# Loading ScalarE's activation tables ahead, and queueing four SiLUs later, in a one-core decoder layer

## The chip, the cores and the metric

The kernel runs on one core of one Trainium2 chip. The metric is the device time of one execution in microseconds (us): a kernel's time is the median of several runs, and beside it there is one execution taken by the hardware profiler. The core's engines each have an instruction queue of their own that is worked off in order: TensorE (PE, matrix products), VectorE (DVE), ScalarE (ACT, activation functions and copies), GpSimd (POOL) and SyncE (SP, which here issues the DMA transfers). They meet only through semaphores.

## The reference, cut to what matters

One decoder layer over 1024 tokens of width 1024. One input projection gives all streams and a SiLU gate for each of three branches; the gated branches go through one output projection and a layer norm.

```python
z = x @ w_in[layer]
u_a, v_a, g_a, x_b, g_b, q_x, g_x = jnp.split(z, SPLITS, axis=-1)
y_a = spatial_gating(gelu(u_a), gelu(v_a), ...)
y_b = s5_branch(x_b, ...)                       # state-space layer; sin/cos tables, gelu, sigmoid
y_x = memory_cross_attention(q_x, mem, w_k, w_v)   # softmax over 256 memory tokens
y = concatenate([y_a * silu(g_a), y_b * silu(g_b), y_x * silu(g_x)])
x = layer_norm(DN_ALPHA * x + y @ w_out[layer], ln_g[layer], ln_b[layer])
```

Seven streams, then: sin, silu, exp, gelu and sigmoid are all computed on ScalarE, at different times.

## The kernel before

Every large product is done as three fp32r products: each operand is split into a high part, cast by ScalarE (`S.copy`, line 65), and a low part, the rest, subtracted by VectorE (line 62). `piece` loads 256 KB of a weight into a `raw` buffer (4 of them, `NRAW`) and splits it into a `hi` and a `lo` buffer (6 of each, `NPC`).

The order of the work is fixed in two ways. TensorE's order is always that of the program text. For VectorE, ScalarE and GpSimd there are two kinds of stretches, opened by `ordered`: in an "a" stretch these three also keep the order of the text among themselves; in a "p" stretch the tool that builds the program orders them from a simulated timeline, and what is written in a "p" stretch may also be queued ahead of instructions of the "a" stretch before it. SyncE's issues are always ordered by that tool. Small generators (`spawn`, `launch`, `tick`) interleave the side work in the text.

The stages that matter here, in order:

1. The gate of the attention branch (`gx`, four PSUM banks of pool `psu`) and the queries (`q`, four banks of pool `psz`) are computed together over eight k-steps (lines 526 to 546, an "a" stretch). Beside them `ssm_params` prepares the state-space parameters, with two Sin activations (lines 432, 433). In the last step `kv.fetch()` splits the first two pieces of the memory weights (`wk`, `wv` twice), and as soon as a gate is complete, SiLU moves it from PSUM into `yx` (line 544). Then `q_evac` moves the queries: ScalarE writes the upper copy, VectorE the rest (lines 247 and 250).
2. The memory keys and values (`KV.run`, lines 277 to 307) use the same four `psu` banks that SiLU has emptied. From here on it is a "p" stretch. There are four weight pieces of `wk` and `wv`; the third and fourth are split while the products run.
3. The products `xb` and `gb` run while 16 attention units (`s_unit`, lines 560 to 615) are interleaved with them: scores `s`, the negated row maximum `nm` (VectorE), Exp (ScalarE, line 576), the reciprocal `ri` and the scaling (VectorE, lines 580 and 582), transposes `pt` (TensorE, line 587), their split (ScalarE and VectorE), and for each pair of units the product `av`, whose half is copied to `ot` by ScalarE (line 611). `gb` is moved to `yb` as it is (line 222), and `gb_silu` (line 805) applies SiLU to it in place later in the text, after the attention's end.
4. The remaining products (`v`, `u`, `ga`), the state-space batches, the output projection and the layer norm follow.

ScalarE holds one set of function tables at a time. The program builder puts an ACT_TABLE_LOAD ahead of an activation whose function isn't in the set that is loaded; the trace shows these loads as instructions of ScalarE, with the line of the activation that they serve. Plain copies and casts run under any set.

Of the kernel before, what the change touches and what calls it, by code (L numbers as in the profile page):

```python
# [9 lines left out]
F32 = mybir.dt.float32  # L10
# [3 lines left out]
AF = mybir.ActivationFunctionType  # L14
# [4 lines left out]
P = 128  # L19
# [17 lines left out]
def trunk_kernel(ctx, tc, xT, x, w_gq, w_kv, memT, w_fm, w_v, w_o,  # L37
# [3 lines left out]
    V, S, G, T = nc.vector, nc.scalar, nc.gpsimd, nc.tensor  # L41
# [6 lines left out]
    def ordered(kind):  # L48
        order_st.close()
        if sets[kind]:  # L50
            order_st.enter_context(tc.manual_schedule(engines=set(sets[kind])))
# [3 lines left out]
    def mul(eng, o, a, b):  # L55
        eng.tensor_tensor(o, a, b, op=ALU.mult)
# [11 lines left out]
    def open_pool(name, bufs=1, side="left", space=None):  # L68
        st = ExitStack()
        kw = dict(name=name, bufs=bufs)  # L70
        if space is not None:
            kw["space"] = space
        else:
            kw["side"] = side
        return st, st.enter_context(tc.tile_pool(**kw))

    dram_st, dpool = open_pool("xd", space=bass.MemoryType.DRAM)
    const_st, const = open_pool("const")
# [29 lines left out]
    def advance():  # L108
        while pending and gate[0] <= now[0]:
            gen, spacing = pending.pop(0)  # L110
            gate[0] = max(gate[0], now[0] - 4.0) + spacing
            active.append([now[0], gen])
        for job in list(active):
            if job[0] <= now[0]:
                lag = next(job[1], None)
                if lag is None:
                    active.remove(job)
                else:
                    job[0] = now[0] + lag

    def tick(cost):
        now[0] += cost
        advance()
# [18 lines left out]
    def mm3(ps, sh, sl, mh, ml, start, stop, chk=False):  # L142
        kw = dict(skip_group_check=True) if chk else {}
        T.matmul(ps, lhsT=sh, rhs=mh, start=start, stop=False, **kw)  # L144
        T.matmul(ps, lhsT=sh, rhs=ml, start=False, stop=False, **kw)  # L145
        T.matmul(ps, lhsT=sl, rhs=mh, start=False, stop=stop, **kw)  # L146
# [13 lines left out]
    yb = base.tile([P, 2, SEQ], F32, tag="yb", name="yb")  # L160
    tok = [slice(t * P, t * P + P) for t in range(8)]
    half = [slice(0, 512), slice(512, 1024)]
# [59 lines left out]
        return lambda h, ps: S.copy(dst[:, f, half[h]], ps)  # L222


    warm = const.tile([P, P], BF16, name="warm")
    V.memset(warm, 0.0)
    wps = zbank("warm")
# [14 lines left out]
    def q_evac():  # L242
        for f in range(2):
            for h in range(2):
                for hh in range(2):
                    src = qps[f][h][hh * 64:hh * 64 + 64]
                    S.activation(qs[0:64, 2 * f + hh, half[h]], src, AF.Copy, scale=0.125)
                for hh in range(2):
                    src = qps[f][h][hh * 64:hh * 64 + 64]
                    V.scalar_tensor_tensor(qs[64:128, 2 * f + hh, half[h]], src, 0.125,  # L250
                                           qs[0:64, 2 * f + hh, half[h]].bitcast(F32),
                                           op0=ALU.mult, op1=ALU.subtract)
# [96 lines left out]
    def ssm_params():  # L349
# [81 lines left out]
        yield 3.0  # L431
        S.activation(sn, ang, AF.Sin, scale=TWO_PI)
        S.activation(an2, ang, AF.Sin, scale=PI_LO)
        mul(V, an2, an2, an2)
        V.tensor_scalar(cn, an2, -2.0, 1.0, op0=ALU.mult, op1=ALU.add)
        yield 3.0
# [35 lines left out]
    kv = KV()  # L472
# [42 lines left out]
    def first_half(wt):  # L515
        def mm(f, w, x, a, b, start=False):
            T.matmul(fps[f][0][:, a:b], lhsT=wt[f][w], rhs=(xh, xl)[x][:, 0, a:b], start=start,
                     stop=False, skip_group_check=True)

        for w, x in ((0, 0), (1, 0), (0, 1)):  # L520
            for m, (a, b) in enumerate(cuts):
                mm(0, w, x, a, b, w + x + m == 0)
        for w, x in ((0, 0), (0, 1), (1, 0)):
            mm(1, w, x, 0, 512, w + x == 0)

    wts = [stage(0)]
    for kt in range(KT):
        wt = wts[kt]
        if kt < KT - 1:
            wts.append(stage(kt + 1))  # L530
        if kt == KT - 1:
            kv.fetch()
        for f in range(4):
            wh, wl = wt[f]
            if kt == 0 and f < 2:
                if f == 0:
                    first_half(wt)
                mm3(fps[f][1], wh, wl, xh[:, 0, half[1]], xl[:, 0, half[1]], True, False)
            else:
                mm3x2(fps[f], wh, wl, kt, kt == 0, kt == KT - 1,  # L540
                      skip=(0,) if f < 2 else ())
            if kt == KT - 1 and f < 2:
                for h in range(2):
                    S.activation(yx[:, f, half[h]], fps[f][h], AF.Silu)
        if kt < KT - 1:
            tick(5.2)
    q_evac()
    ordered("p")
    tick(5.2)
    run_units([kv], xb[0])  # L550
# [5 lines left out]
    ordered("p")  # L556
    att_st, att = open_pool("att", side="right")
    pts = {}

    def s_unit(lt, hp):  # L560
        ps = ubank(f"s{lt}{hp}")
        for hh in range(2):
            qt = qs[:, 2 * hp + hh, tok[lt]]
            pv = ps[:, hh * 256:hh * 256 + 256]
            T.matmul(pv, lhsT=qt, rhs=kh[:, 2 * hp + hh], start=hh == 0, stop=False,
                     skip_group_check=True)
            T.matmul(pv, lhsT=qt, rhs=kl[:, 2 * hp + hh], start=False, stop=hh == 1,
                     skip_group_check=True)
        now[0] += 0.43
        ps3 = ps.rearrange("p (h m) -> p h m", h=2)  # L570
        nm = att.tile([P, 2], F32, tag="nm", bufs=3, name=f"nm{lt}{hp}")
        V.tensor_reduce(nm, ps3, axis=AX.X, op=ALU.max, negate=True)
        pr = att.tile([P, 2, 256], F32, tag="pr", bufs=3, name=f"pr{lt}{hp}")
        rs = att.tile([P, 2], F32, tag="rs", bufs=3, name=f"rs{lt}{hp}")
        for h in range(2):
            S.activation(pr[:, h], ps3[:, h], AF.Exp, bias=nm[:, h:h + 1], scale=1.0,
                         accum_out=rs[:, h:h + 1])
        yield 2.5
        ri = att.tile([P, 2], F32, tag="ri", bufs=3, name=f"ri{lt}{hp}")
        V.reciprocal(ri, rs)  # L580
        for h in range(2):
            V.tensor_scalar(pr[:, h], pr[:, h], ri[:, h:h + 1], None, op0=ALU.mult)
        yield 1.3
        tp = ubank(f"pt{lt}{hp}")
        for h in range(2):
            for m in range(2):
                T.transpose(tp[:, (h * 2 + m) * P:(h * 2 + m) * P + P],
                            pr[:, h, m * P:m * P + P], ident)
        now[0] += 0.43
        lq, lr = lt // 2, lt % 2  # L590
        if lr == 0:
            pts[(lq, hp)] = (att.tile([P, 4, 256], F32R, tag="pth", bufs=2, name=f"pth{lq}{hp}"),
                             att.tile([P, 4, 256], F32R, tag="ptl", bufs=2, name=f"ptl{lq}{hp}"))
        ph, pl = pts[(lq, hp)]
        tp3 = tp.rearrange("p (a l) -> p a l", a=4)
        S.copy(ph[:, :, tok[lr]], tp3)
        sub(V, pl[:, :, tok[lr]], tp3, ph[:, :, tok[lr]].bitcast(F32))
        if lr == 1:
            yield 3.8
            ps = ubank(f"av{lq}{hp}")  # L600
            for h in range(2):
                for m in range(2):
                    for n, pp in enumerate((ph, pl)):
                        T.matmul(ps[:, h * 256:h * 256 + 256], lhsT=vs[:, m, 2 * hp + h],  # L604
                                 rhs=pp[:, h * 2 + m], start=h + m + n == 0,
                                 stop=h + m + n == 3, skip_group_check=True)
            now[0] += 0.87
            cs = slice(lq * 256, lq * 256 + 256)
            ot = att.tile([P, 256], F32, tag="ot", bufs=2, name=f"ot{lq}{hp}")
            for h in range(2):  # L610
                S.copy(ot[h * 64:h * 64 + 64], ps[64:128, h * 256:h * 256 + 256])
            for h in range(2):
                add(V, ot[h * 64:h * 64 + 64], ps[0:64, h * 256:h * 256 + 256],
                    ot[h * 64:h * 64 + 64])
            mul(V, yx[:, hp, cs], yx[:, hp, cs], ot)
# [22 lines left out]
    for hp in range(2):  # L638
        for lt in range(8):
# [7 lines left out]
                  lambda tt, ps, vb=vb: v_evac(vb, tt, ps), lambda vb=vb: v_done(vb))  # L647
# [157 lines left out]
    def gb_silu():  # L805
        for f in range(2):
            for h in range(2):
                S.activation(yb[:, f, half[h]], yb[:, f, half[h]], AF.Silu)
                yield 2.0

    gate[0] = now[0]
# [22 lines left out]
    def v_done(vb):  # L834
        spawn(mix_all(vb))
# [158 lines left out]
    for t in range(7):  # L994
        ps = zbank(f"o1{t}")
# [6 lines left out]
    for c in range(2):  # L1002
        ps = zbank(f"o17{c}")
# [86 lines left out]
```

## Time and profile before

| what | value |
|---|---|
| median of the runs | 397.46 us (3 runs: 397.12 to 398.84) |
| profiled execution | 398.77 us |
| its span, first to last instruction | 397.1 us |
| busy: PE, DVE, ACT, POOL | 381.8, 267.6, 158.2, 101.2 us |
| mean granted TensorE clock | 0.994 of full speed |

The profiled execution's own time is 1.67 us longer than its span, and 1.31 us above the median of the runs. Busy times add up instructions of one engine; the engines overlap. In the rows below, the number in brackets is the idle time of the engine before the instruction, with what ended it.

### The profile page before, as it was taken

To read this page: it belongs to the slowest core of one execution; us is meant where nothing else is said; L and a number is where in the kernel's file an instruction comes from. 1 tells how busy PE (TensorE), PEld (TensorE's weight loads), DVE (VectorE), ACT (ScalarE), POOL (GpSimd) and SP (SyncE) were. 2 spreads that over 40 slices of the span, in tenths; PEclk is the share of its full clock that TensorE was granted. 3 is DMA by queue.
4 is the path that set the end of the run, shared out by engine and by line. 5 is a ranking of instruction groups with operands and counts; after the bars stand their busy time and mean duration, and the time that the engine had idled before them with its cause. 6 is when DMAs were issued, how large, how long until landed. Compare 5 with 4: busy or idle time off the path is not lost.

```text
span 397.1 us, 5806 instructions
## 1 busy us (share of the span) xinstructions
PE 381.8 (96%) x2129; PEld 330.2 (83%) x2129; DVE 267.6 (67%) x579; ACT 158.2 (40%) x301; POOL 101.2 (25%) x80
## 2 busy tenths in 40 slices
PE   8999989899998999999999999999999999999990
PEld 7887888688886999888888999888888888888890
DVE  4579877788885778799769349754447311874475
ACT  4572496576778432323153223134356310012210
POOL 1305000000000493830954600310000000026773
PEclk9999999999999999999999999999999999999997
DMA  7873525221850100302011002400138710002124
GB/s 230 286 242 117 164 80 185 82 79 28 152 62 26 54 4 14 107 24 71 28 42 56 26 17 82 132 0 2 53 104 295 290 55 0 0 2 88 70 107 159
DMA packets 22189, 35.89 MB, mean 90 GB/s; under 512 B 5376, under 2 KB 8848, under 8 KB 22032
## 3 DMA queue, kind: packets, MB, share of 16 engines
q1 hardware_dynamic: 22160, 35.51, 29.3%
q8 instruction: 17, 0.28, 0.3%
q14 instruction: 12, 0.10, 0.1%
HBM read 29.67 MB, written 5.24 MB: 88 GB/s over the span
## 4 chain that ended last, share of the span: by engine, by line
PE 77%; DVE 7%; DMA 7%; ACT 5%; issue 2%; POOL 2%; SPq 0%; POOLq 0%; DVEq 0%; ACTq 0%
PE o L146 7%; PE o L145 7%; PE o L144 7%; DMA r_x<-in_xT_dram 5%; PE zv L146 4%; PE zv L145 4%; PE zv L144 4%; PE zu L151 4%; PE zu L152 4%; PE zg L151 4%; PE zu L154 4%; PE zg L152 4%; PE zg L154 4%; PE mx L858 2%; PE av L604 2%
## 5 line engine op out<-in xcount | busy, mean ns | idle before, releaser
L928 POOL TENSOR_TENSOR stat<-stat,nhalf 128x1 f32<-128x1 f32 x8 | 11.9, 1490 | 105.6 <-DVE stat L927 105.6
L146 PE MATMUL o<-h_wo,yl 128*128 128x512 f32 (+1 forms) x100 | 38.4, 384 | 0.0
L145 PE MATMUL o<-l_wo,yh 128*128 128x512 f32 (+1 forms) x100 | 38.4, 384 | 0.0
L144 PE MATMUL o<-h_wo,yh 128*128 128x512 f32 (+1 forms) x100 | 38.3, 383 | 0.0
L144 PE MATMUL zv<-h_v,xh 128*128 128x256 f32 x128 | 36.6, 286 | 0.0
L146 PE MATMUL zv<-h_v,xl 128*128 128x256 f32 x128 | 36.2, 283 | 0.0
L145 PE MATMUL zv<-l_v,xh 128*128 128x256 f32 x128 | 36.2, 283 | 0.0
L151 PE MATMUL zu<-xh,h_u 128*128 128x512 f32 x64 | 25.8, 404 | 0.0
L151 PE MATMUL zg<-xh,h_g 128*128 128x512 f32 x64 | 25.5, 399 | 0.0
L152 PE MATMUL zu<-xl,h_u 128*128 128x512 f32 x64 | 25.0, 391 | 0.0
L152 PE MATMUL zg<-xl,h_g 128*128 128x512 f32 x64 | 25.0, 390 | 0.0
L144 PEld LDWEIGHTS zv<-h_v,xh 128*128 128x128 f32 x128 | 24.5, 192 | 0.1
L145 PEld LDWEIGHTS zv<-l_v,xh 128*128 128x128 f32 x128 | 24.5, 192 | 0.1
L146 PEld LDWEIGHTS zv<-h_v,xl 128*128 128x128 f32 x128 | 24.5, 192 | 0.0
L937 ACT ACTIVATE res<-res,stat 128x1024 f32<-128x1024 f32 x6 | 6.9, 1157 | 41.1 <-POOL stat L928 41.1
L956 DVE SCALAR_TENSOR_TENSOR res<-res,o 128x512 f32<-128x512 f32 (+1 forms) x16 | 10.3, 646 | 19.2 <-PE o L146 19.2
L145 PEld LDWEIGHTS o<-l_wo,yh 128*128 128x128 f32 x100 | 18.8, 188 | 4.0
L144 PEld LDWEIGHTS o<-h_wo,yh 128*128 128x128 f32 x100 | 18.8, 188 | 3.9
L146 PEld LDWEIGHTS o<-h_wo,yl 128*128 128x128 f32 x100 | 18.8, 188 | 3.9
L154 PE MATMUL zu<-xh,l_u 128*128 128x512 f32 x64 | 19.8, 390 | 0.0
L154 PE MATMUL zg<-xh,l_g 128*128 128x512 f32 x64 | 19.7, 389 | 0.0
L665 POOL MEMSET M<- 128x512 f32 x2 | 1.0, 526 | 70.1 <-PE zgb L152 70.1
(300 smaller groups left out, 1077.9 us busy)
## 6 DMA issues: line engine op xcount, KB each, us to landing
r_wo<-in_w_o_dram SPq DMA_DIRECT2D x16, 256.0 KB, 2.9
res<-in_x_dram SPq DMA_DIRECT2D x8, 512.0 KB, 7.5
r_x<-in_xT_dram SPq DMA_DIRECT2D x15, 256.0 KB, 5.1
out_dram<-res SPq DMA_DIRECT2D x6, 512.0 KB, 2.6
r_v<-in_w_v_dram SPq DMA_DIRECT2D x8, 256.0 KB, 3.0
r_u<-in_w_fm_dram SPq DMA_DIRECT2D x8, 256.0 KB, 2.7
r_g<-in_w_fm_dram SPq DMA_DIRECT2D x8, 256.0 KB, 2.7
r_wgq<-in_w_gq_dram SPq DMA_DIRECT2D x7, 256.0 KB, 4.5
```

The lines of the kernel that those rows point to most:

```text
L144: T.matmul(ps, lhsT=sh, rhs=mh, start=start, stop=False, **kw)
L145: T.matmul(ps, lhsT=sh, rhs=ml, start=False, stop=False, **kw)
L146: T.matmul(ps, lhsT=sl, rhs=mh, start=False, stop=stop, **kw)
L151: T.matmul(ps[h], lhsT=wh, rhs=xh[:, kt, half[h]], start=first, stop=False, **kw[h])
L152: T.matmul(ps[h], lhsT=wh, rhs=xl[:, kt, half[h]], start=False, stop=False, **kw[h])
L154: T.matmul(ps[h], lhsT=wl, rhs=xh[:, kt, half[h]], start=False, stop=last, **kw[h])
L604: T.matmul(ps[:, h * 256:h * 256 + 256], lhsT=vs[:, m, 2 * hp + h], rhs=pp[:, h * 2 + m], start=h + m + n == 0, stop=h + m + n == 3, skip_ ...
L665: G.memset(t, 0.0)
L858: T.matmul(ps[:, tok[c]], lhsT=t[:, cq * 4 + c, tok[h]], rhs=wT[:, hd], start=(c == 0), stop=(c == 3), skip_group_check=True)
L928: G.tensor_tensor(rs, rs, nhalf[:, 0:1], op=ALU.pow)
L937: S.activation(ot, ot, AF.Copy, scale=rs)
L956: V.scalar_tensor_tensor(res[:, t, c0:c0 + w], res[:, t, c0:c0 + w], ALPHA, ps[:, :w], op0=ALU.mult, op1=ALU.add)
```

## The change

A two-column constant tile `dummy` and a helper `table(func)` are added: `table` runs one activation from the first column into the second, one element on each partition. It is called twice: with Silu, right behind the two Sin activations of `ssm_params`, and with Exp, right behind `q_evac` and still in the "a" stretch. In the last k-step only the first piece of the memory weights is split; the second follows behind the four SiLUs, ahead of `q_evac`. The four SiLUs of `g_b` get an edge in ScalarE's queue behind the last copy to `ot` of the attention.

```diff
+    dummy = const.tile([P, 2], F32, name="dummy")
+    V.memset(dummy, 0.0)
+
+    def table(func):
+
+        S.activation(dummy[:, 1:2], dummy[:, 0:1], func)
...
         S.activation(an2, ang, AF.Sin, scale=PI_LO)
+        table(AF.Silu)
...
         if kt == KT - 1:
-            kv.fetch()
+            kv.fetch(1)
...
             tick(5.2)
+    kv.fetch(2)
     q_evac()
+    table(AF.Exp)
     ordered("p")
...
+    last_att = [None]
...
             for h in range(2):
-                S.copy(ot[h * 64:h * 64 + 64], ps[64:128, h * 256:h * 256 + 256])
+                last_att[0] = S.copy(ot[h * 64:h * 64 + 64], ps[64:128, h * 256:h * 256 + 256])
...
             for h in range(2):
-                S.activation(yb[:, f, half[h]], yb[:, f, half[h]], AF.Silu)
+                with tc.issue_after(last_att[0].ins):
+                    S.activation(yb[:, f, half[h]], yb[:, f, half[h]], AF.Silu)
                 yield 2.0
```

## Rows read from the trace of the kernel before

**Rows 1.** All of TensorE's waits: for whom, us in total, times, longest.

```profile
PE pt L587 <- DVE pr L582: 2.9, 2, 1.8
PE k L144 <- ACT yx L544: 1.2, 1, 1.2
PE warm L229 <- DVE warm L226: 1.1, 1, 1.1
PE gx L152 <- DVE xl L62: 0.3, 1, 0.3
PE k L146 <- DVE l_wk L62: 0.2, 1, 0.2
```

**Rows 2.** Timeline of TensorE: start us, us, instruction, idle before.

```profile
44.46 0.39 PE L151 MATMUL gx<-xh,h_wgq 128*128 128x512 f32 x1
...
51.30 0.38 PE L144 MATMUL k<-mh,h_wk 128*128 128x256 f32 x1 [1.24 <-ACT yx L544]
...
76.45 0.70 PE L587 MATMUL pt<-ident,pr 128*128 128x128 f32 x4 [1.17 <-DVE pr L582]
...
125.17 0.63 PE L587 MATMUL pt<-ident,pr 128*128 128x128 f32 x4 [1.76 <-DVE pr L582]
```

**Rows 3.** Timeline of ScalarE, 39 to 58 us.

```profile
39.25 1.14 ACT L65 CAST xh<-r_x 128x512 fp32r<-128x512 f32 x2
...
48.71 0.62 ACT L65 CAST h_wk<-r_wk 128x512 fp32r<-128x512 f32 x1 [3.24 <-PE q L154]
49.35 1.28 ACT L544 ACT_TABLE_LOAD   x1
50.65 2.07 ACT L544 ACTIVATE yx<-gx 128x512 f32<-128x512 f32 x4
52.57 2.43 ACT L247 ACTIVATE qs<-q 64x512 fp32r<-64x512 f32 x4
...
57.87 0.61 ACT L65 CAST h_wk<-r_wk 128x512 fp32r<-128x512 f32 x1
```

**Rows 4.** The chain that ended last, 60 to 77 us: start, us, what.

```profile
60.91 2.73 DMA r_xb<-in_w_fm_dram
...
72.82 0.61 DVE nm L572
...
73.50 1.28 ACT L576
...
76.05 0.36 DVE pr L582
```

**Rows 5.** Timeline of ScalarE, 119 to 142 us.

```profile
119.66 1.28 ACT L808 ACT_TABLE_LOAD   x1
120.96 1.16 ACT L808 ACTIVATE yb<-yb 128x512 f32<-128x512 f32 x2
122.12 1.28 ACT L576 ACT_TABLE_LOAD   x1
...
131.91 0.75 ACT L611 COPY ot<-av 64x256 f32<-64x256 f32 x2 [2.97 <-PE av L604]
...
140.46 1.28 ACT L827 ACT_TABLE_LOAD   x1 [2.05 <-issue]
```

**Rows 6.** Timeline of VectorE: the row maximum of the last attention unit.

```profile
118.75 0.69 DVE L572 TENSOR_REDUCE nm<-s 128x2 f32<-128x512 f32 x1
```

**Rows 7.** ScalarE's instructions grouped by line: busy us, mean ns, idle before.

```profile
L576 ACT ACTIVATION_READ_ACCUMULATOR pr<-s,nm 128x1 f32 x32 | 6.4, 200 | 0.0
```

**Rows 8.** Timeline of VectorE, 41 to 61 us.

```profile
41.72 1.29 DVE L62 TENSOR_TENSOR xl<-r_x,xh 128x512 fp32r<-128x512 f32 x2
...
53.81 2.80 DVE L250 SCALAR_TENSOR_TENSOR qs<-q,qs 64x512 fp32r<-64x512 f32 x4 [2.29 <-ACT qs L247]
...
60.19 0.69 DVE L62 TENSOR_TENSOR l_wk<-r_wk,h_wk 128x512 fp32r<-128x512 f32 x1
```

**Rows 9.** Busy time of each engine in one stretch of the attention.

```profile
79.00:100.00 21.00, 21.00 (x131) 18.53 (x130) 18.13 (x44) 15.59 (x47) 0.00 (x0) 1.00 0.18 56
```

## The prediction

> **What bounds the kernel now.** I first read the list of what TensorE waits for. TensorE is busy for 381.8 of 397.1 us, and this list is complete and short [rows 1]: besides the start-up there are four waits, together 4.6 us, all before 126 us. From there until the output's tail TensorE has no wait. So this change can only win those few microseconds, and whatever it removes from them early arrives in full at the end, as long as nothing new makes TensorE wait.
>
> Next, TensorE's timeline says where they are [rows 2]: 1.24 us before the first key product (51.30), 1.17 us before the first transposes (76.45), and 1.76 us before the last attention unit's transposes (125.17). ScalarE's timeline and the chain then show what stands behind each. At the first, ScalarE casts a weight piece, loads the Silu table and only then frees the banks that the key products need [rows 3]. At the second, an Exp table load of 1.28 us lies between the row maximum and the Exp [rows 4]. At the third, the last Exp stands behind a Silu load, two SiLUs of `g_b` and another Exp load, 3.74 us in all [rows 5]. The change aims at all three.
>
> **Part 1, the Exp table ahead: 1.17 us.** The load at 73.50 is removed from the path, so Exp, reciprocal and scaling come 1.28 us earlier; the scaled rows, now done at 76.05 + 0.36 = 76.41, are done at 75.13 [rows 4]. TensorE has been free since 76.45 - 1.17 = 75.28 [rows 2], so the whole 1.17 us go, with 0.15 to spare.
>
> The load now stands behind `q_evac`, with its one-element activation. No row shows such an activation. From below it is nothing; from above a full SiLU, 2.07 / 4 = 0.52 us [rows 3]; the nearest row is another instruction of one element a partition, 0.20 us [rows 7], and I take that. Queued behind are the casts of the fourth `wk` and `wv`: the cast at 57.87 moves by 1.28 + 0.20 to 59.35 and ends at 59.96 [rows 3]. VectorE doesn't take that piece up before 60.19 [rows 8], because it is still busy with `qs`. So it costs nothing, by a margin of 0.23 us; with the upper price, 0.09.
>
> Here a rule has to be weighed. From the end of the cast before the Silu load (48.71 + 0.62) to the first SiLU (50.65) it is 1.32 us, of which 1.28 are the load [rows 3]. The Trainium skill (ScalarE: Activation LUTs, What ACT_TABLE_LOAD costs) puts a switch at 2.66 us, a load of 1.28 and a drain of 1.38; the trace agrees with the load and has no room for the drain. By its figure the fourth `wk` cast would end at about 61.3, over a microsecond behind VectorE, and the sum would be 1.8 instead of 2.9 us, by an estimate from that page.
>
> **Part 2, the `g_b` SiLUs behind the attention: 1.76 us.** The row maximum of the last unit is ready at 118.75 + 0.69 = 119.44 [rows 6], so without the 3.74 us Exp starts at 119.66. From the end of the second load (123.40) to TensorE's restart it is 1.77 us [rows 2, 5]; TensorE could have its rows at 121.4 and comes for them at 125.17 - 1.76 = 123.41. The whole wait goes, with 2 us to spare. The four SiLUs move behind the copy at 131.91: in the old time 132.66 + 1.28 + 4 x 0.58 = 136.3, still ahead of the Gelu load at 140.46 [rows 5]. The move past the copies of `gb` costs TensorE nothing, as only two of the four `psz` banks hang on them and the next products start in the other two. One of the Silu loads and the Exp reload vanish.
>
> **Part 3, the Silu table ahead and the later split: 0 net, out of 1.24 us.** The load is moved to behind the Sin activations. It and the small activation put 1.48 us before the casts of the last k-step's weights and `xh`, which ended at 39.25 + 1.14 = 40.39 [rows 3], now 41.9. VectorE's `xl` splits begin at 41.72 and end at 43.0 [rows 8] and move by a few tenths at most; TensorE comes for the step at 44.46 [rows 2]. Over a microsecond of cover is left; without it, each microsecond would cost one. The `memset` of `dummy` is 0.1 us ahead of TensorE's warm-up [rows 1] and costs nothing.
>
> Then it matters where the third `wk` cast (48.71) stands. It is written behind the SiLUs, in a freely ordered stretch, and yet is queued ahead of them [rows 3]. What made it ready early isn't touched by the change: its raw buffer comes free from the first `wk` split, and `hi` buffers are plentiful if the second piece is held back. So I expect it to stay ahead. The queue is then: that cast, ended at 49.33; four SiLUs until 51.40; the two casts of the second piece, now behind them, until 52.64; then `q_evac`, which started at 52.57 before. TensorE's bank is free at 49.85, and it starts its key products when the last query product is done, at 51.30 - 1.24 = 50.06. That is 1.24 us early, and the second piece (split done by about 53.3) is in time for it.
>
> But `q_evac` hasn't moved, so VectorE's `qs` (53.81) and its split of the fourth `wk`, until 60.88, haven't moved either [rows 8]. TensorE already waited 0.2 us for that split [rows 1]. It will now wait about 1.4 us there: the 1.24 us are given back at the fourth weight piece. And the chain goes on from this split, not from TensorE: its raw buffer lets the next `xb` transfer go at 60.91, and from it come the casts, the keys and the row maximum at 72.82 [rows 4]. The fourth piece's own transfers now wait for the second piece's split, until about 53.3, and land within 2.7 us or so [rows 4], before the cast at 59.35. The two waits on which parts 1 and 2 rest keep their size.
>
> **The sum.** 0 + 1.17 + 1.76 = 2.93 us. Against the profiled execution, 398.77 (span 397.1), that is 395.8 (span 394.2). That execution stood 1.31 us above the median of the runs, so the median goes from 397.46 to **394.5**.
>
> **Rivals.**
>
> *The third cast gets out of the way.* If the later split pushes it behind the SiLUs, these run as soon as the gates are complete, well before 50.06, and `q_evac` can start near 50 instead of 52.57. VectorE's chain up to the row maximum then moves by up to 2.5 us, and the first wait, the 0.2 us one and the 1.17 all go: 1.24 + 0.2 + 1.17 + 1.76 = 4.37, a time of 393.1; with banks freed at once rather than 0.52 us apart, half a microsecond less, 392.6. For it: it is what a held back second piece would do if buffers were handed out in the order of the text. Against: the reasons above. A third `wv` cast that also jumps ahead stays with my forecast within 0.3 us.
>
> *Only one of the two later waits goes.* The row maximum may be queued later in VectorE's new order, or the cast behind the Exp load may come after VectorE is ready for it (the margin is 0.23 us). Then one has 1.76 and little else: 395.7, or 0.44% less, hardly to be told from no change.
>
> *A switch costs more than its load.* If the first work behind a load were held up once more for about as long as the load took, the fourth `wk` cast would end 1.28 us later, at 61.24 instead of 59.96, and VectorE's split would start 1.05 us late: 395.5. Against it is the 1.32 us from cast to SiLU [rows 3]. The drain that the Trainium skill (ScalarE: Activation LUTs, What ACT_TABLE_LOAD costs) adds to each load would be such a case.
>
> *Slower: VectorE falls behind in the attention.* Between 51 us and the end of the attention VectorE's queue is ordered anew by the tool, and it is busy for 18.13 of 21.00 us there [rows 9]. If in the new order a weight split of 0.69 us goes before the row maximum of every second one of the 16 units and isn't absorbed, TensorE waits 8 x 0.69 = 5.5 us more: 397.46 - 2.93 + 5.5 = 400.0. It eats up the gain from 0.18 us a unit, and makes the kernel slower by 0.5% from 0.31 us a unit. Against it: TensorE doesn't wait once in this stretch now, and no instruction of the units changes.
>
> **How the numbers follow.** My forecast gets 0.47, the third cast out of the way 0.25, cases between these two 0.09, only one of the later waits 0.10, the dearer switch 0.03, slower 0.06. Leaving out the tails, the range goes from 392.6 to 395.9. Half a per cent (2.0 us) is about what a measurement here tells from no change: faster by more than that 0.80, within it 0.14, slower 0.06.
>
> **What would show it.** In the profile of the changed kernel: Silu load near 38 us, Exp load before 60 us, neither at the SiLUs of `gx` nor between a row maximum and Exp; one Silu load after the last `ot` copy; no TensorE wait at the first and the last transposes; the key products starting at about 50, and a wait of over a microsecond for the fourth `wk` split. If that last wait is missing and `q_evac` starts near 50, the first rival holds. I am wrong if the Exp load is repeated, if the fourth `wk` split is later than 61, or if new waits of `pt` for scaled rows appear.

## The result, and the profile after

The changed kernel takes 391.75 us (5 runs: 391.06 to 393.15) against 397.50 (5 runs: 397.12 to 398.84) of the kernel before on the same chip: a ratio of 0.9858, 95% interval 0.984 to 0.9875, which is 5.6 us less (5.0 to 6.4). That is faster, as forecast, but by nearly twice the forecast 2.9 us, and 0.85 us below the low end of the range. The profiled execution took 391.75 us, with a span of 389.9. One execution of split_only below took 640 us and one of no_split 2172 us; the ratios leave them out.

TensorE's waits, all of them, by whom, us in total, times, longest (the changed kernel; they answer to [rows 1]):

```profile
PE warm L236 <- DVE warm L233: 1.1, 1, 1.1
PE gx L145 <- DVE xl L62: 0.6, 1, 0.6
PE gx L144 <- ACT xh L511: 0.2, 1, 0.2
```

The two waits of `pt` and the two of `k` are gone, and none has come in their place. What is left belongs to the start-up. In particular the wait of over a microsecond for the fourth `wk` split, which the prediction expected, is missing.

ScalarE's timeline shows why (start, us, instruction, idle before and its releaser; it answers to [rows 3, 5]):

```profile
36.75 1.28 ACT L230 ACT_TABLE_LOAD   x1
38.04 0.20 ACT L230 ACTIVATE dummy<-dummy 128x1 f32<-128x1 f32 x1
...
45.51 1.09 ACT L552 ACTIVATE yx<-gx 128x512 f32<-128x512 f32 x2 [4.14 <-PE gx L154]
46.87 1.09 ACT L552 ACTIVATE yx<-gx 128x512 f32<-128x512 f32 x2 [0.27 <-PE gx L154]
47.84 0.62 ACT L65 CAST h_wk<-r_wk 128x512 fp32r<-128x512 f32 x1
48.35 0.63 ACT L65 CAST h_wv<-r_wv 128x512 fp32r<-128x512 f32 x1
48.87 0.63 ACT L65 CAST h_wk<-r_wk 128x512 fp32r<-128x512 f32 x1
49.39 2.42 ACT L254 ACTIVATE qs<-q 64x512 fp32r<-64x512 f32 x4
...
54.78 1.28 ACT L230 ACT_TABLE_LOAD   x1
56.08 0.20 ACT L230 ACTIVATE dummy<-dummy 128x1 f32<-128x1 f32 x1
56.19 0.60 ACT L65 CAST h_wk<-r_wk 128x512 fp32r<-128x512 f32 x1
...
70.20 0.47 ACT L587 ACTIVATE pr<-s,nm 128x256 f32<-128x256 f32 x1 [3.13 <-DVE nm L583]
...
115.58 0.47 ACT L587 ACTIVATE pr<-s,nm 128x256 f32<-128x256 f32 x1
...
125.87 0.75 ACT L622 COPY ot<-av 64x256 f32<-64x256 f32 x2 [2.96 <-PE av L615]
126.64 1.28 ACT L820 ACT_TABLE_LOAD   x1
127.93 1.15 ACT L820 ACTIVATE yb<-yb 128x512 f32<-128x512 f32 x2
...
130.58 1.16 ACT L820 ACTIVATE yb<-yb 128x512 f32<-128x512 f32 x2
134.40 1.28 ACT L839 ACT_TABLE_LOAD   x1 [2.66 <-issue]
```

Ahead of the SiLUs of `gx` there is neither a load nor a weight cast. They are released by the gates themselves (45.51 and 46.87); the second piece's two casts follow, and behind those the third `wk` cast, which stood ahead of the SiLUs at 48.71 before. `q_evac` starts at 49.39 instead of 52.57. Further down, neither Exp shown has a load in front of it, and the SiLUs of `g_b` stand behind the last `ot` copy; the last of them ends at 130.58 + 1.16 = 131.74, 2.7 us ahead of the Gelu load.

VectorE's timeline shows what `q_evac` brings with it (answers to [rows 8]):

```profile
50.62 2.80 DVE L257 SCALAR_TENSOR_TENSOR qs<-q,qs 64x512 fp32r<-64x512 f32 x4 [0.23 <-ACT qs L254]
...
57.01 0.69 DVE L62 TENSOR_TENSOR l_wk<-r_wk,h_wk 128x512 fp32r<-128x512 f32 x1
```

`qs` starts at 50.62 instead of 53.81, and the fourth `wk` split, which the prediction kept at 60.19, starts at 57.01. The cast behind the Exp load ends at 56.19 + 0.60 = 56.79, so 0.22 us ahead of VectorE.

Where the time came from is read from TensorE's stretches: the windows run from the first key product to the first `xb` product, and from there to the first transposes (engines PE, PEld, DVE, ACT, POOL busy, then granted clock, DMA share, GB/s). First the kernel before:

```profile
51.30:63.66 12.36, 12.18 (x96) 11.75 (x97) 8.93 (x14) 8.73 (x16) 0.00 (x0) 1.00 0.27 82
63.66:76.45 12.79, 11.63 (x54) 8.94 (x52) 9.17 (x20) 9.45 (x23) 0.21 (x1) 1.00 0.54 167
```

and the changed kernel:

```profile
49.62:60.99 11.37, 11.37 (x97) 11.37 (x96) 9.48 (x15) 9.06 (x16) 0.00 (x0) 1.00 0.50 151
60.99:72.42 11.43, 11.43 (x55) 9.18 (x54) 9.53 (x22) 7.83 (x23) 0.20 (x1) 1.00 0.58 174
```

The first stretch is 0.99 us shorter, the second 1.36; TensorE now has no gap in either, at the full granted clock both times. The stretch after them, from the first transposes to the first product of stream `v` (134.48 before, 128.42 after), shrinks from 58.03 to 56.00 us, 2.03 less. With the 1.24 us wait that lay ahead of the key products, this makes 1.24 + 0.99 + 1.36 + 2.03 = **5.62 us**, the size of the measured 5.6. The spans differ by more, 7.2 us: the queries ended 0.44 us earlier in this execution (49.62 against 51.30 - 1.24 = 50.06), and 1.1 us lie behind the first `v` product. The same columns for the window from there to the end, before and then after:

```profile
134.48:397.06 262.58, 253.04 (x1425) 220.65 (x1423) 166.60 (x331) 75.23 (x118) 90.45 (x64) 0.99 0.21 70
128.42:389.93 261.51, 252.56 (x1425) 220.74 (x1423) 166.54 (x331) 74.50 (x119) 90.45 (x64) 0.99 0.21 70
```

These 1.1 us are no accident of the old execution. By the table below (span minus `zv`), this tail is 261.5 us in all nine profiles of kernels that have the `dummy` tile, and 262.0 to 262.7 us in the four that don't, two of them of the kernel before. About 0.5 us of it is in TensorE's products, busy for 253.0 and 252.6 us at the same count; up to 0.6 lies behind the last product, where split_only, though it has no `dummy`, is as short as the nine. Why was not tested. So that 5.62 meets 5.6 is partly luck: the sum leaves this tail out, and it holds a first wait that the kernel before doesn't pay in every execution (before_again, below; against that profile the stretches give only 0.35 + 1.31 + 1.98 = 3.64 us).

### The profile page after: what moved, and what is told of

Its sections match the earlier page's. It is cut to its first block, busy times and chain, and to the rows that moved or that the text cites. A ratio compares the mean times of both kernels' runs of the same rounds, so it can differ in the third digit from the quotient of the medians.

```text
span 389.9 us, 5809 instructions
## 1 busy us (share of the span) xinstructions
PE 379.0 (97%) x2129; PEld 329.8 (85%) x2129; DVE 267.5 (69%) x580; ACT 155.0 (40%) x301; POOL 101.1 (26%) x80
## 4 chain that ended last, share of the span: by engine, by line
PE 94%; POOL 2%; issue 1%; DMA 1%; DVE 1%; SPq 0%; POOLq 0%; ACT 0%
PE o L146 7%; PE o L145 7%; PE o L144 7%; PE zv L145 4%; PE zv L144 4%; PE zv L146 4%; PE zu L152 4%; PE zu L151 4%; PE zg L152 4%; PE zg L151 4%; PE zu L154 4%; PE zg L154 4%; PE av L615 2%; PE zgb L152 2%; PE zgb L154 2%; PE zxb L152 2%
```

## The experiments

Two theories stood against each other at the start. *Order* ("queue theory" in the texts below): the later split pushed the third `wk` cast behind the SiLUs, and this starts ScalarE's and VectorE's queues about 3 us earlier; the early Silu load alone is then worth little. *Load* ("table theory"): the early Silu load did it, by taking 1.28 us out of the path ahead of the SiLUs, and the split only changes places. For reading the runs, this table has the starts, in us, of the first key product, the first `xb` product, the first transposes and the first `v` product, each from one profiled execution, and that execution's span:

| kernel | `k` | `zxb` | `pt` | `zv` | span |
|---|---|---|---|---|---|
| before | 51.30 | 63.66 | 76.45 | 134.48 | 397.1 |
| before_again | 50.09 | 61.81 | 74.55 | 132.53 | 395.2 |
| split_only | 48.89 | 60.28 | 72.51 | 130.51 | 392.5 |
| silu_only | 49.35 | 61.66 | 74.46 | 132.48 | 394.0 |
| exp_only | 50.82 | 63.18 | 74.69 | 132.72 | 394.2 |
| gb_only | 51.41 | 63.78 | 76.52 | 132.58 | 395.0 |
| no_split_again | 50.13 | 61.50 | 72.93 | 128.93 | 390.4 |
| no_split_third | 49.09 | 61.05 | 72.50 | 128.58 | 390.1 |
| no_silu | 49.15 | 60.53 | 71.95 | 127.95 | 389.5 |
| no_silu_again | 49.03 | 60.41 | 71.83 | 127.83 | 389.3 |
| after | 49.62 | 60.99 | 72.42 | 128.42 | 389.9 |
| after_again | 48.97 | 60.34 | 71.77 | 127.77 | 389.3 |
| exp_thrice | 49.06 | 62.77 | 74.38 | 130.46 | 392.0 |

**One part at a time, on the kernel before.** The later split alone (split_only):

```diff
         if kt == KT - 1:
-            kv.fetch()
+            kv.fetch(1)
...
+    kv.fetch(2)
     q_evac()
```

> The kernel before with one edit: the second memory weight piece is split behind the SiLUs of gx. Queue theory (the third wk cast, queued ahead of these SiLUs and waiting for its transfer, is what held them; the later split moves it behind): SiLUs start with the gates near 46 us, the Silu load runs before them in ScalarE's idle time, the key products follow the last query product without a wait, about 1.9 us are won there and part of the 1.17 us of the next wait, as VectorE's chain is earlier: 394.7 to 395.6. Table theory (the Silu load ahead of the SiLUs is what held them): the load still stands there and costs its 1.28 us, 396.8 to 397.5.

Measured: 394.41 against 397.21 us, ratio 0.9932 (0.9911 to 0.9953), 2.7 us less (1.9 to 3.5): the order theory's side, a little more than it said. ScalarE's timeline of split_only:

```profile
39.72 1.28 ACT L544 ACT_TABLE_LOAD   x1
...
44.78 1.09 ACT L544 ACTIVATE yx<-gx 128x512 f32<-128x512 f32 x2 [3.79 <-PE gx L154]
...
47.12 0.62 ACT L65 CAST h_wk<-r_wk 128x512 fp32r<-128x512 f32 x1
...
48.67 2.42 ACT L247 ACTIVATE qs<-q 64x512 fp32r<-64x512 f32 x4
```

Nothing was loaded ahead here by the program, and still the SiLUs go as soon as the gates are complete. The Silu load, still tied to line 544, has run by itself at 39.72, and ScalarE was then idle for 3.79 us until the gates were complete. The key products have no wait. TensorE's waits of split_only say what else went:

```profile
PE pt L588 <- DVE pr L583: 2.4, 2, 1.8
```

Of the wait at the first transposes 0.67 us are left, of 1.17: an earlier row maximum pays a part of the Exp load.

The early Silu load alone (silu_only; the `dummy` tile and the helper come with it, here and in exp_only):

```diff
         S.activation(an2, ang, AF.Sin, scale=PI_LO)
+        table(AF.Silu)
```

> The kernel before with one edit: the Silu table loaded behind the Sin activations. Queue theory: the third wk cast still ends near 49.3, SiLUs from there, key products at 50 but fed bank by bank, query copies 1.2 us earlier; 1.2 to 1.4 us won, 396.1 to 396.3. Table theory: the whole first wait and all that hangs on it goes, 1.9 us or more, 395.6 or less.

Measured: 395.30 against 397.21, ratio 0.9946 (0.9929 to 0.9963), 2.1 us less (1.5 to 2.8). By its time the run meets the load theory's forecast and not the order theory's. ScalarE's timeline of silu_only:

```profile
48.14 0.62 ACT L65 CAST h_wk<-r_wk 128x512 fp32r<-128x512 f32 x1 [2.94 <-DMA r_wk<-in_w_kv_dram]
48.66 2.05 ACT L552 ACTIVATE yx<-gx 128x512 f32<-128x512 f32 x4
50.58 2.42 ACT L254 ACTIVATE qs<-q 64x512 fp32r<-64x512 f32 x4
```

The third cast still stands ahead of the SiLUs, and what it waits for is its own transfer. The load that stood between them is gone, and the SiLUs start 0.52 us behind the cast instead of 1.94. But by the table only the first wait went: from `k` on the stretches are 12.31, 12.80 and 58.02 us, against 12.36, 12.79 and 58.03 before, and the rest of the difference between the two profiles is the start and the 1.1 us tail. So either part moves the queue, the split further (`q_evac` at 48.67) than the load (50.58).

The Exp table ahead alone (exp_only) and the late `g_b` SiLUs alone (gb_only), both on the kernel before:

```diff
     q_evac()
+    table(AF.Exp)
```
```diff
+    last_att = [None]
...
-                S.copy(ot[h * 64:h * 64 + 64], ps[64:128, h * 256:h * 256 + 256])
+                last_att[0] = S.copy(ot[h * 64:h * 64 + 64], ps[64:128, h * 256:h * 256 + 256])
...
+                with tc.issue_after(last_att[0].ins):
+                    S.activation(yb[:, f, half[h]], yb[:, f, half[h]], AF.Silu)
```

> The kernel before with one edit: the Exp table loaded behind the query copies. My step: the wait of 1.17 us before the first transposes goes and nothing else, 395.8 to 396.1. Dearer switch (a load holds the next work up twice): the fourth wk split is a microsecond late and takes most of it back, 396.8 to 397.2.

> The kernel before with one edit: the four SiLUs of g_b queued behind the last copy of the attention. My step: the wait of 1.76 us before the last unit's transposes goes, with a slow restart of up to 0.2 us, 395.2 to 395.5. Rival: the SiLUs block the copies of gb and the next stage's casts behind them and part comes back, 396 or more.

Measured: exp_only 395.39 against 397.09, ratio 0.9961 (0.9948 to 0.9973), 1.55 us less, a little more than forecast; gb_only 395.17, ratio 0.9954 (0.9938 to 0.997), 1.8 us less, as forecast. The waits of exp_only, and then of gb_only:

```profile
PE pt L595 <- DVE pr L590: 1.7, 1, 1.7
PE k L144 <- ACT yx L551: 1.3, 1, 1.3
```

```profile
PE k L144 <- ACT yx L544: 1.4, 1, 1.4
PE pt L588 <- DVE pr L583: 1.1, 1, 1.1
```

Each part takes its own wait and leaves the others as they were. These are the prediction's parts 1 and 2, as it described them. In its profile exp_only has the shorter tail as well; 1.28 us in the stretch and 1.1 there would be 2.4, so the medians need not hold all of that tail.

**One part out of the changed kernel.** The first piece of `fetch` made whole again (no_split, no_split_again and no_split_third), and the early Silu load left out (no_silu, no_silu_again):

```diff
-            kv.fetch(1)
+            kv.fetch()
...
-    kv.fetch(2)
     q_evac()
```
```diff
         S.activation(an2, ang, AF.Sin, scale=PI_LO)
-        table(AF.Silu)
```

> The changed kernel with the second memory weight piece split where it was before. Queue theory: third wk cast ahead of the SiLUs again, key products fed bank by bank at 0.52 us, query copies from 51.4 instead of 49.4; 0.7 to 1.5 us slower than the changed kernel, 392.5 to 393.3. Table theory: no difference, 391.8.

> The changed kernel without the Silu activation behind the Sin ones. Queue theory: the load that the SiLUs need finds ScalarE idle between the first weight piece and the gates and costs nothing, 391.8. Table theory: the load comes back onto the path, 393.0 or more.

Measured: no_split 392.43 against 397.21, ratio 0.988 (0.9859 to 0.9901); no_silu 391.12, ratio 0.9841 (0.9823 to 0.9858), and in a second set (no_silu_again) 391.09, ratio 0.9854 (0.9835 to 0.9874). no_split was measured again, on one chip with the changed kernel:

> The changed kernel with the second memory weight piece split where it was before, once more, for a profile that can be read. Queue theory: third wk cast ahead of the SiLUs, waiting for its transfer until 48 or later, key products without a full stop but fed bank by bank, query copies about 1.2 us later than in the changed kernel and a wait at the fourth weight piece; about 392.4. Rival (VectorE bound, the same whichever order): no wait of TensorE at the key products, the loss of 1 us somewhere else.

> The changed kernel itself, beside the others on one chip. If the early Silu load is worth nothing once the second piece is split later, it stands with the kernel without that load, 391.0 to 391.8; if it is worth its own 1.28 us, it is at 390.0 or less.

no_split_again took 392.62 against 397.09, ratio 0.9909 (0.9882 to 0.9936), and after_again 391.37, ratio 0.9866 (0.9848 to 0.9885). So without the split about 1 us is lost (392.4 and 392.6 against 391.75 and 391.4; both pairs go the same way, though their intervals overlap), less than the split is worth alone. Without the early Silu load no loss is seen: 391.1 twice. ScalarE's timeline of no_silu:

```profile
40.90 1.28 ACT L551 ACT_TABLE_LOAD   x1
...
45.04 1.09 ACT L551 ACTIVATE yx<-gx 128x512 f32<-128x512 f32 x2 [2.86 <-PE gx L154]
```

With nothing ahead of the SiLUs that waits, the load finds ScalarE idle before the gates are complete, and the part is needless.

In the profile of no_split_again TensorE was late in its start-up and met the third cast done, so its stretches are those of the changed kernel and don't show where the microsecond goes. One more execution of it was profiled, and one of the kernel before:

> The changed kernel with the second memory weight piece split where it was before, for one more profile, in which TensorE is less late at the start. Queue theory: TensorE's last query product ends near 49 and the SiLUs, behind the third wk cast, end after that, so that key products wait for banks by up to 0.5 us in all and for the fourth wk split: 12 us from the first key product to the first xb product, against 11.4 in the changed kernel. Rival (no cost of the order): 11.4 us here too.

> The kernel before once more, for a second profile. If the 0.3 us wait of gx at 39 us and the longer tail of the first profile belong to that execution and not to the kernel, this profile has a shorter span (395.0 to 395.8) with the same three waits at the key products, the first and the last transposes.

no_split_third (391.81 us), ScalarE's timeline and then TensorE's waits:

```profile
47.53 0.62 ACT L65 CAST h_wk<-r_wk 128x512 fp32r<-128x512 f32 x1 [2.95 <-DMA r_wk<-in_w_kv_dram]
48.06 2.05 ACT L552 ACTIVATE yx<-gx 128x512 f32<-128x512 f32 x4
49.98 2.42 ACT L254 ACTIVATE qs<-q 64x512 fp32r<-64x512 f32 x4
```

```profile
PE k L146 <- DVE l_wk L62: 0.2, 1, 0.2
```

The SiLUs stand behind the third cast once more and empty the banks from 48.06 on, while TensorE comes for the first at 49.09. It finds that one free, loses a little at a later bank (50.16) and 0.2 us at the fourth split; from its first key product to `zxb` it takes 11.96 us, against 11.37 with the split: 0.6 of the microsecond, in one execution.

before_again (396.92 us), ScalarE's timeline:

```profile
46.86 0.62 ACT L65 CAST h_wk<-r_wk 128x512 fp32r<-128x512 f32 x1 [3.23 <-DMA r_wk<-in_w_kv_dram]
47.50 1.28 ACT L544 ACT_TABLE_LOAD   x1
48.79 2.06 ACT L544 ACTIVATE yx<-gx 128x512 f32<-128x512 f32 x4
```

Here the transfer came early, the first bank was free at about 49.4, the key products started without a wait at 50.09, and the two waits of `pt` were as before. What was expected of this run came true in the span (395.2 us) and missed twice: the first wait is gone, and the longer tail stayed (262.7 us behind `zv`). So the first wait [rows 2] is a race between the third `wk` transfer and TensorE, won or lost with the start-up: the kernel before doesn't pay the 1.24 us in every execution.

**What a switch costs.** In the changed kernel, two more switches behind the Exp load, and the fourth pieces' casts held behind the last (exp_thrice):

```diff
     table(AF.Exp)
+    table(AF.Silu)
+    kv.behind = table(AF.Exp)
...
+                    if kp == 2:
+                        with tc.issue_after(self.behind.ins):
+                            self.one()
```

> The changed kernel with two more table loads (Silu, and Exp again, each with its one-element activation) behind the Exp load that it has, and the fourth wk and wv casts held behind them. If a switch costs its load and the activation, 1.41 us as the changed kernel's trace shows, the fourth cast is 2.8 us later; 0.2 us of that are covered by VectorE and 0.7 by TensorE, so the kernel is 1.8 to 2.0 us slower than the changed one: 393.2 to 393.6. If each switch held the next work up by as much again, 4.5 to 5 us slower, about 396. The output is the reference's.

Measured: 394.17 against 397.30, ratio 0.9931 (0.991 to 0.9952), so 2.4 to 2.8 us more than the changed kernel, where 1.8 to 2.0 were expected: in part because a switch with another load behind it takes 1.52 us and not 1.41. ScalarE's timeline, and TensorE's wait:

```profile
54.23 1.28 ACT L230 ACT_TABLE_LOAD   x1
...
55.75 1.28 ACT L230 ACT_TABLE_LOAD   x1
...
57.26 1.28 ACT L230 ACT_TABLE_LOAD   x1
...
58.66 0.60 ACT L65 CAST h_wk<-r_wk 128x512 fp32r<-128x512 f32 x1
```

```profile
PE k L144 <- ACT h_wk L65: 1.6, 1, 1.6
```

From load to load it is 1.52 and 1.51 us, and 1.40 from the last load to the cast: the load itself and some 0.2 us. A switch that costs twice its load is ruled out here. The run shows the other side of the margin too: with the cast 3.1 us later than in after_again (58.66 instead of 55.54), VectorE and TensorE wait, and `zxb` starts 2.4 us later, 62.77 against 60.34.

## Why the prediction was wrong, point by point

**Part 1 (Exp ahead) held, a little small.** It was sized at the wait, 1.17 us; the stretch lost 1.36, and exp_only alone gained 1.55 (1.1 to 2.1). The load and its 0.20 us activation, priced from another one-element instruction [rows 7], came out as put; from the load to the cast it is 1.41 us, as the two overlap a little. The margin is 0.22 us against 0.23, but by luck: both the cast and the split came 3 us earlier than the prediction had them.

**Part 2 (`g_b` SiLUs late) held, a little small.** Sized at 1.76, the stretch lost 2.03, and gb_only alone gained 1.8. In both parts the excess, 0.19 and 0.27 us, is TensorE time beside its waits. Of the 0.27, 0.10 are seen at the first restart: from the first transposes to the next ones it was 2.41 us behind the wait (76.45 to 78.86) and 2.31 without one (72.42 to 74.73). Nearly all the rest is at the last restart: the start of the last unit's transposes came 1.92 us closer to the product ahead of it, of which 1.76 were the wait.

**Part 3 is the step that failed.** It read "So I expect it to stay ahead" of the third `wk` cast, and from that "`q_evac` hasn't moved", and gave the 1.24 us of the first wait back in full at the fourth weight piece. With the split the cast goes behind the second piece, and `q_evac` moved by 3.2 us. There was no wait at that piece. The term put at 0 was 1.24 + 0.99 = 2.23 us in these two executions, and split_only, by medians, gained 2.7. no_split_third and silu_only show the premise at fault: the third cast stays ahead exactly where the later split is missing, and this holds for all thirteen profiles. The order seen fits the weight pieces being cast in the order of the text: once the second was put behind the SiLUs, the third followed. Why the building tool keeps this order (a shared pool of buffers, or its priorities) was not tested.

There is a second, smaller error in that step. Even with the cast ahead, `q_evac` would not have stayed: in silu_only it came to 50.58, and with the second piece's two casts put before it (1.03 us, 47.84 to 48.87 in the changed kernel) that is some 51.6, a microsecond before 52.57. About 0.4 of it is that the prediction added durations, where in these rows the next cast or activation starts some 0.1 us before the one ahead of it ends (a cast of 0.62 us, the next start 0.52 behind). The rest is that it took the cast's place, 48.71, as fixed from one execution. It is a transfer's landing, plus 0.1 us, between 46.78 and 48.83 in the seven profiles with the cast ahead.

**The first rival** ("the third cast gets out of the way") was right in its mechanism, and its own sign was met: no wait at the fourth split, `q_evac` near 50. Its sum of 4.37, or 4.9 with banks freed at once, missed 5.6 by what the two `pt` stretches gave beyond their waits (0.46) and by the rest of the 0.99 us, of which it had 0.2, or 0.7 with the banks. No sum of the prediction had the tail. That it was given 0.25 and not more rests on an argument about buffers, for which the trace of before had no row.

**Two sums.** The 4.6 us that the prediction gives for four waits are five: the wait of `gx` [rows 1], 0.3 us, is among them, and its own four come to 4.37. The dearer switch, 397.46 - 2.93 + 1.05, gives 395.6 and not 395.5. Neither changes the argument.

**The other rivals** fell. Both later waits went. A switch cost 1.40 to 1.52 us (exp_thrice). VectorE did not fall behind in the attention: TensorE doesn't wait there at all.

**How the parts add.** Alone, the split, Exp and `g_b` give 2.7 + 1.55 + 1.8 = 6.05 us; together, in no_silu, 6.3 and 5.8. Within the noise they add, although the split already takes 0.5 us of the wait that the Exp load made. The split and the early Silu load don't: alone they give 2.7 and 2.1 us, but from the changed kernel the first can be taken for about 1 us and the second for nothing, as each stands in for the other. Either is enough to free the first bank in time; only the split also moves the cast. The simplest version is no_silu: three parts, 391.1 us, not distinguishable from the changed kernel.

## What to carry to other kernels

When a piece of work is moved in the text of a freely ordered stretch, ask which later pieces of the same kind will follow it in the queue, and work out the sum for both orders: here a step put at nothing gained 2.7 us by itself. Before loading a table ahead, look whether ScalarE is idle between the last use of the old set and the first of the new: the load may run in that gap by itself, as Silu's did here and Exp's did not, and then what is to be removed is the work queued in front. A wait that hangs on a transfer's landing is a race; look at more than one execution before counting it in full. And when the stretches are added up, compare the part of the program that was not meant to change, too.

## What was unexpected of the hardware

A table load does not always wait with its activation. In split_only it ran at 39.72 while the SiLU it served started at 44.78, and in no_silu at 40.90 for 45.04; the Exp load of the kernel before, however, started only at the end of the row maximum [rows 4], though ScalarE was idle:

```profile
73.50 1.28 ACT L576 ACT_TABLE_LOAD   x1 [3.02 <-DVE nm L572]
```

The trace has a difference between them: a semaphore wait stands in ScalarE's queue directly ahead of this load, and none ahead of the two early ones, whose wait comes with the activation. This fits that the wait's place decides when a load runs. Why it was put ahead of the one and not of the others was not tested.

In exp_thrice, three switches in a row took 1.40 to 1.52 us each, the one-element activation included. The Trainium skill (ScalarE: Activation LUTs, What ACT_TABLE_LOAD costs) adds a drain of about 1.38 us to each load; no profile here shows it.

The start-up moves by itself: between executions TensorE ended the queries anywhere from 48.9 to 50.1 us, with the whole program behind it moved along. That 1.2 us may be a good part of the scatter of the kernel before, 395.85 to 398.75 us in 22 runs of one chip; those runs have no profile that would show it.
